# Modulating x instead of the weights and biases, loading the first operands by halves, and summing the gate row four slices at a time

## The chip, the cores and the metric

One core of a Trainium2 chip runs the whole layer. The metric is device time in microseconds (us), the median over several executions; the trace is one further execution under the hardware profiler.

## The reference

One hybrid decoder layer on x (4096 x 1024), cut to what matters here:

```
shift, scale, gate = split(silu(c) @ W_ada + b_ada)      # three rows of 1024
h = x * (1 + scale) + shift                              # adaLN modulation
p = h @ W_in                                             # W_in is 1024 x 3712
u = gelu(p[:, 0:512]); v = gelu(p[:, 512:1024]); g = p[:, 1024:1536]
A = u * (causal mix over chunks of 128 of groupwise LayerNorm(v)) * silu(g)
r, k, v, gate_b, wd, ad = token_shift(p[:, 1536:])       # t + mu * (previous t - t)
B = rwkv7(r, k, v, wd, ad) * silu(gate_b)
y = LayerNorm(alpha * x + gate * (concat(A, B) @ W_out))
```

## The kernel before

x comes transposed (xT), so that a matmul contracts over the 1024 features, in eight slices of 128 (KD = 8). Time is cut into 16 blocks of 256 steps (T). Each float32 operand is split into a rounded high part (ScalarE copy, L258) and the remainder (GpSimd or VectorE subtract, L259), and a product takes several matmuls: `gemm` (L381) makes per slice one of 128x512 (high weight against both halves of x) and one of 128x256 (low weight against high x); `added` (L390) joins the two sums.

The work has three stages. **Stage A** (`group_a`, 16 blocks) makes from x the parts that need no recurrence: four blocks of u, two half blocks of v (`psv`, L619 to L621), four of g (`w_g`), four of the gate of B (`w_gb`), one of decay and rate (`w_wd`), and at the end the spatial mix (`pM`, L667), whose results leave through `oa` (L672, L675). While a block runs, generators are advanced beside it (`alongside`): `weights` for block 0; `ada_gate`, which sums the gate row, for blocks 1 and 2; `stash`, which prepares later weights and puts them into DRAM, from block 3; `load_b` for block 15. **Stage B** runs the recurrence over two groups of heads, its order on the engines written out by `Weave`; it reads back the split x that stage A stored (`xhl`). The last stage multiplies by W_out (`pso`).

In stage A the order of instructions on each engine, the SyncE DMA queue included, is set by the framework before the run, from program order and modelled readiness; buffers of one tag are handed out in rotation. The tags that matter: `st` in `hpool` (3 buffers: loads of x, weights, gate slices), `wst` in `apool` (3), `w` in `w2` (6 of 8 KB per partition), `hl` in `hpool` (5: split x).

The modulation is never applied to x. `mod` holds shift in columns 0 to 7 and 1 + scale in columns 8 to 15. Each weight block is multiplied by 1 + scale on load (L285, L422, L533/534, L559), and shift times the weights becomes a bias: `group_row` (L340) sums a slice with a weight of 32 columns, on one quarter of the array's columns for each k % 4, `set_bias` (L261) turns that row into a column, and the bias goes into the activations (L400, L601, L642, L863) or is added (`bvb`, L624). At the beginning the four 1 MB loads of `w_ada` for scale come first, then W_in for u and x; those for shift come after the u products have begun. `ada_gate` loads one 128x512 slice of `w_ada` a step and sums the one before it.

Of the kernel before, what the change touches and what calls it, by code (L numbers as in the profile page):

```python
# [209 lines left out]
def hybrid_layer(ctx: ExitStack, tc: tile.TileContext, x, xT, w_ada, b_gate, w_in, cols,  # L210
# [43 lines left out]
    bias = cp_.tile([P, 25], F32, name="bias")  # L254
# [14 lines left out]
    def fetch_w(c0, name, nb, pool=None, eng=g, pools=None):  # L269
# [10 lines left out]
        def finish():  # L280
            pq = ps_m.tile([P, P], F32, tag="m", name="pbias")
            for q, st in enumerate(sts):
                for k in range(4):
                    group_row(pq, mod, 4 * q + k, st[:, k])
                v.tensor_tensor(st, st, mod[:, 8 + 4 * q:12 + 4 * q].unsqueeze(2).to_broadcast([P, 4, P]), op=ALU.mult)  # L285
                split(w[:, 0, 4 * q:4 * q + 4], w[:, 1, 4 * q:4 * q + 4], st, eng)
            set_bias(nb, pq)
            if nb >= 8:
                v.tensor_tensor(halo[:, nb - 8:nb - 7], omm[:, nb - 8:nb - 7], bias[:, nb:nb + 1], op=ALU.mult)
# [8 lines left out]
    def load_parts(src, i, keep=None):  # L298

        parts = []  # L300

        def quarters():
            kept = []
            for q in range(4):
                st = hpool.tile([P, 2, T], F32, tag="st", name="hst", bufs=3)
                ld(st, src[q * 256:(q + 1) * 256, i * T:(i + 1) * T].rearrange("(k p) t -> p k t", p=P))
                hl = hpool.tile([P, 2, 2, T], F32R, tag="hl", name="hx")
                split(hl[:, 0], hl[:, 1], st)
                parts.extend(hl[:, :, k] for k in range(2))
                kept.append(hl)  # L310
                yield
            if keep is not None:
                for q, hl in enumerate(kept):
                    ld(keep[:, q], hl.bitcast(F32))

        return parts, quarters()
# [29 lines left out]
    def ada_gate():  # L346
        for q in range(2):
            qs = slice(q * 512, (q + 1) * 512)
            pq = ps_l.tile([P, 512], F32, tag="l", name="pq")
            gst = []  # L350

            def fetch(k):
                st = hpool.tile([P, 512], F32, tag="st", name="gst", bufs=3)
                ld(st, w_ada[k * P:(k + 1) * P, 2 * D + q * 512:2 * D + (q + 1) * 512])
                gst.append(st)
# [18 lines left out]
    def load_all(src, i, keep=None):  # L374
        parts, steps = load_parts(src, i, keep)
        for _ in steps:
            pass
        return parts


    def gemm(h, w, spare=False):  # L381
        shape = [P, 2, T]
        ps = ps_s.tile(shape, F32, tag="s", name="psd") if spare else ps_d.tile(shape, F32, tag="d", name="psd")
        for k in range(KD):
            both = h[k]
            pe.matmul(ps, w[:, 0, k], both, start=(k == 0), stop=(k == KD - 1), skip_group_check=True)  # L386
            pe.matmul(ps[:, 0], w[:, 1, k], both[:, 0], start=False, stop=(k == KD - 1), skip_group_check=True)  # L387
        return ps
# [7 lines left out]
    def shift(ps, blk, pool, dst):  # L396
# [3 lines left out]
        s.activation(pv[:, 1:T + 1], ps, AF.Identity, scale=col(V_MU, blk), bias=bias[:, 8 + blk:9 + blk])  # L400
# [10 lines left out]
    def stash():  # L411
        for p in range(2):
            for nm, o in (("k", 512), ("r", 0), ("v", 1024)):
                c0 = o + (2 + p) * P
                pq = ps_m.tile([P, P], F32, tag="m", name="pbias")
                for q in range(2):
# [3 lines left out]
                    for k in range(4):  # L420
                        group_row(pq, mod, 4 * q + k, st[:, k])
                    v.tensor_tensor(st, st, mod[:, 8 + 4 * q:12 + 4 * q].unsqueeze(2).to_broadcast([P, 4, P]), op=ALU.mult)  # L422
                    stash_parts(wps[nm, p], q, st.rearrange("p k c -> p (k c)"))
                    yield
                later_bias(8 + c0 // P, pq)
# [17 lines left out]

    def later_bias(nb, pq):
        set_bias(nb, pq)
        v.tensor_tensor(halo[:, nb - 8:nb - 7], omm[:, nb - 8:nb - 7], bias[:, nb:nb + 1], op=ALU.mult)
# [17 lines left out]
    def load_b(ph):  # L464

        late = None
        for p in range(2):
            for nm, o in (("k", 512), ("r", 0), ("v", 1024)):
                c0 = o + (2 * ph + p) * P
                R[ph, nm, p], fin_ = fetch_w(NA + c0, f"w_{nm}{p}", 8 + c0 // P)  # L470
                if late:
                    late()
                late = fin_
                yield
# [11 lines left out]
    with ExitStack() as actx:  # L486
# [4 lines left out]
        bvb = apool.tile([P, DA], F32, name="bvb", bufs=1)  # L491
# [24 lines left out]
        wa = [ada_cols(2), ada_cols(3)]  # L516
        ust = []
        for r in range(2):
            t_ = w2.tile([P, KD, 256], F32, tag="w", name=f"ust{r}")
            ld(t_, w_in[:, r * 256:(r + 1) * 256].rearrange("(k p) c -> p k c", p=P))  # L520
            ust.append(t_)
            if r == 0:
                x0 = load_all(xT, 0, xhl[0])
        for n in range(2):
            ada_sum(2 + n, wa[n])
        v.scalar_tensor_tensor(mod[:, 8:16], pm[:, 8:16], 1.0, V[:, V_BA + 8:V_BA + 16], op0=ALU.add, op1=ALU.add)
        wa = [ada_cols(0), ada_cols(1)]

        def u_block(b):
            st = ust[b // 2][:, :, (b % 2) * P:(b % 2 + 1) * P]  # L530
            w = wpool.tile([P, 2, KD, P], F32R, tag="w", name=f"w_u{b}")
            for k in range(KD):
                s.activation(w[:, 0, k], st[:, k], AF.Copy, scale=mod[:, 8 + k:9 + k])  # L533
                v.scalar_tensor_tensor(w[:, 1, k], st[:, k], mod[:, 8 + k:9 + k], w[:, 0, k].bitcast(F32),
                                       op0=ALU.mult, op1=ALU.subtract)
            wu.append(w)

        def weights():
            for b in range(4):
                u_block(b)  # L540
                yield
            for n in range(2):
                ada_sum(n, wa[n])
            v.tensor_tensor(mod[:, 0:8], pm[:, 0:8], V[:, V_BA:V_BA + 8], op=ALU.add)
            for b in range(4):
                pq = ps_m.tile([P, P], F32, tag="m", name="pbias")
                for k in range(KD):
                    group_row(pq, mod, k, ust[b // 2][:, k, (b % 2) * P:(b % 2 + 1) * P])
                set_bias(b, pq)
# [5 lines left out]
            pvb = ps_l.tile([P, DA], F32, tag="l", name="pvb")  # L555
            for k in range(KD):
                st = vst[k // 4][:, k % 4]
                group_row(pvb, mod, k, st)
                v.tensor_scalar(st, st, mod[:, 8 + k:9 + k], None, op0=ALU.mult)  # L559
# [738 lines left out]
```

## Time and profile before

| | |
|---|---|
| median of 3 runs | 2567.16 us (2561.15 to 2572.73) |
| the profiled execution's own time | 2566.92 us |
| its span in the trace | 2565.2 us |
| TensorE matmuls busy | 2426.9 us, 95% of the span |
| VectorE, ScalarE, GpSimd busy | 62%, 50%, 30% |
| the 16 blocks of stage A end (last `pM` begins) | 916.87 us |

Busy TensorE time counts overlapping matmuls by their modelled ends, so 95% is not 95% of its peak.

### The profile page before, as it was taken

The numbers are of one execution on the slowest core, as the hardware profiler recorded it, in microseconds if no ns is written. First come the engines' busy times: TensorE is split into PE (matmuls) and PEld (weight loads), VectorE is DVE, ScalarE is ACT, GpSimd is POOL, SyncE is SP. The second block draws the span as 40 slices with busy tenths as digits, with TensorE's granted clock in tenths as the row PEclk, the third lists the DMA queues.
The fourth block names the chain that finished last, engine by engine and source line by source line (L and its number), as shares of the span: only waits on it lengthen the run. The fifth ranks groups of instructions, "written<-read, shape, count | busy, mean of one in ns | idle before, by whom it ended". The sixth has DMA issues, their size and how long they took to land.

```text
span 2565.2 us, 58841 instructions
## 1 busy us (share of the span) xinstructions
PE 2426.9 (95%) x23144; PEld 2095.7 (82%) x23144; DVE 1585.1 (62%) x4222; ACT 1277.6 (50%) x2963; POOL 768.3 (30%) x1419
## 2 busy tenths in 40 slices
PE   6999999999999989999999989999999998899998
PEld 3767888888888878888888888888988887688887
DVE  3733444434344457878778877778877787555555
ACT  3524444444443456676666656766766665211111
POOL 1412233322221242333233333333333333222221
PEclk8999999999999999999999999999999999999999
DMA  8423434543232252222122252222221224344442
GB/s 283 140 91 114 140 135 165 176 162 136 77 120 84 79 156 76 84 68 88 59 80 88 63 178 84 63 84 72 75 84 55 88 79 150 104 148 148 140 148 99
DMA packets 183102, 286.21 MB, mean 112 GB/s; under 512 B 14500, under 2 KB 125220, under 8 KB 181032
## 3 DMA queue, kind: packets, MB, share of 16 engines
q1 hardware_dynamic: 182824, 282.44, 33.7%
q8 instruction: 182, 2.98, 0.5%
q14 instruction: 96, 0.79, 0.1%
HBM read 188.00 MB, written 94.38 MB: 110 GB/s over the span
## 4 chain that ended last, share of the span: by engine, by line
PE 50%; DVE 15%; ACT 7%; issue 3%; DMA 2%; POOL 1%; SPq 0%; DVEq 0%; ACTq 0%; POOLq 0%
PE pso L1250 13%; PE psd L166 12%; PE psd L386 6%; PE pU L166 3%; PE pC L166 3%; PE psd L387 3%; PE pA L166 2%; DVE big L166 2%; DVE X L166 2%; DVE tmp L166 2%; PE pY L166 1%; PE pt L166 1%; DVE S L166 1%; PE pG L166 1%; ACT pv L166 1%
## 5 line engine op out<-in xcount | busy, mean ns | idle before, releaser
L1250 PE MATMUL pso<-wo,hx 128*128 128x512 f32 x1440 | 330.1, 391 | 1.8 <-POOL hx L1250 1.3
L1250 PEld LDWEIGHTS pso<-wo,hx 128*128 128x128 f32 x1440 | 270.3, 188 | 60.2 <-POOL hx L1250 1.7
L166 PE MATMUL psd<-hx,w_v 128*128 128x256 f32 x1512 | 248.9, 291 | 8.2 <-DVE kt L166 5.5
L166 PE MATMUL psd<-hx,w_r 128*128 128x256 f32 x1512 | 249.7, 290 | 1.1 <-DVE kt L166 1.1
L166 PE MATMUL psd<-hx,w_k 128*128 128x256 f32 x1512 | 238.9, 299 | 5.2 <-DVE rt L166 5.1
L393 DVE TENSOR_TENSOR sum<-psd,sum 128x256 f32<-128x256 f32 x208 | 87.5, 421 | 205.1 <-ACT sum L392 204.7
L166 PEld LDWEIGHTS psd<-hx,w_v 128*128 128x128 f32 x1512 | 202.9, 190 | 13.7 <-DVE kt L166 7.0
L166 PEld LDWEIGHTS psd<-hx,w_k 128*128 128x128 f32 x1512 | 203.0, 198 | 8.2 <-DVE rt L166 6.7
L166 PEld LDWEIGHTS psd<-hx,w_r 128*128 128x128 f32 x1512 | 203.7, 190 | 4.3 <-DVE kt L166 1.7
L386 PE MATMUL psd<-hx,w_u 128*128 128x512 f32 x512 | 188.4, 410 | 6.8 <-POOL hx L259 6.8
L386 PE MATMUL psd<-hx,w_gb 128*128 128x512 f32 x512 | 182.6, 397 | 2.9 <-DVE sum L393 2.9
L386 PE MATMUL psd<-hx,w_g 128*128 128x512 f32 x512 | 183.6, 400 | 0.9 <-DVE vg L624 0.4
L1250 POOL TENSOR_TENSOR hx<-hst,hx 128x512 fp32r<-128x512 f32 x58 | 84.2, 1452 | 219.2 <-ACT hx L1250 217.3
L166 ACT ACTIVATE pv<-psd,bias,V 128x256 f32<-128x256 f32 x192 | 106.4, 564 | 79.9 <-PE psd L166 77.4
L387 PE MATMUL psd<-hx,w_u 128*128 128x256 f32 x512 | 145.4, 285 | 0.0
L387 PE MATMUL psd<-hx,w_gb 128*128 128x256 f32 x512 | 143.9, 281 | 0.0
L387 PE MATMUL psd<-hx,w_g 128*128 128x256 f32 x512 | 143.7, 281 | 0.0
L392 ACT COPY sum<-psd 128x256 f32<-128x256 f32 x208 | 76.0, 366 | 118.8 <-PE psd L387 118.7
L166 POOL COPY halo<-pv 128x1 f32<-128x1 f32 x192 | 40.2, 210 | 309.4 <-ACT pv L166 302.9
L1250 DVE SCALAR_TENSOR_TENSOR z<-z,pso 128x512 f32<-128x512 f32 x60 | 41.2, 686 | 146.8 <-PE pso L1250 146.7
L386 PEld LDWEIGHTS psd<-hx,w_u 128*128 128x128 f32 x512 | 98.4, 193 | 35.6 <-POOL hx L259 10.0
L386 PEld LDWEIGHTS psd<-hx,w_g 128*128 128x128 f32 x512 | 96.1, 188 | 30.5 <-issue 5.1
(309 smaller groups left out, 5947.5 us busy)
## 6 DMA issues: line engine op xcount, KB each, us to landing
hx<-xhl SPq DMA_DIRECT2D x126, 512.0 KB, 4.1
xhl<-hx SPq DMA_DIRECT2D x64, 512.0 KB, 3.0
hst<-in_xT_dram SPq DMA_DIRECT2D x64, 256.0 KB, 3.1
hst<-oT SPq DMA_DIRECT2D x64, 256.0 KB, 2.9
z<-in_x_dram SPq DMA_DIRECT2D x32, 512.0 KB, 3.6
out_dram<-z SPq DMA_DIRECT2D x32, 512.0 KB, 2.6
wst<-in_w_in_dram SPq DMA_DIRECT2D x42, 256.0 KB, 3.0
wa<-in_w_ada_dram SPq DMA_DIRECT2D x8, 1024.0 KB, 9.5
```

The source lines that it names most:

```text
L166: fn(*a, **k)
L386: pe.matmul(ps, w[:, 0, k], both, start=(k == 0), stop=(k == KD - 1), skip_group_check=True)
L387: pe.matmul(ps[:, 0], w[:, 1, k], both[:, 0], start=False, stop=(k == KD - 1), skip_group_check=True)
L392: s.copy(t_, ps[:, 1])
L393: v.tensor_tensor(t_, ps[:, 0], t_, op=ALU.add)
L1250: fn(*a, **k)
```

## The change

x is multiplied by 1 + scale and shift is added, in place, before it is split (`modulate`: one `tensor_scalar` for each of the two slices of a quarter of x). The weights are split as they are, and every bias, `set_bias`, `later_bias`, the group rows for biases and `bvb` are gone; `pv` becomes a Copy with a scale. The start loads by halves of the contraction: `first_half(a)` loads scale and shift for 512 features, two quarters of x and 512 rows of the u weights; `second_half(a)` splits them, sums scale and shift and modulates. The four u products run over slices 0 to 3, and after the second half over 4 to 7. In `group_a` the g products come ahead of the v products. `ada_gate` loads four slices in one step and sums all four in the next.

```diff
-    def set_bias(nb, pq):
-        rows = hpool.tile([P, P], F32, tag="rows", name="brow", bufs=1)
-        s.copy(rows, pq)
-        pb_ = ps_m.tile([P, 1], F32, tag="m", name="pb_")
-        pe.matmul(pb_, rows, row32, start=True, stop=True)
-        v.tensor_copy(bias[:, nb:nb + 1], pb_)
...
         def finish():
-            pq = ps_m.tile([P, P], F32, tag="m", name="pbias")
             for q, st in enumerate(sts):
-                for k in range(4):
-                    group_row(pq, mod, 4 * q + k, st[:, k])
-                v.tensor_tensor(st, st, mod[:, 8 + 4 * q:12 + 4 * q].unsqueeze(2).to_broadcast([P, 4, P]), op=ALU.mult)
                 split(w[:, 0, 4 * q:4 * q + 4], w[:, 1, 4 * q:4 * q + 4], st, eng)
-            set_bias(nb, pq)
...
+    def modulate(q, st):
+        for k in range(2):
+            c = 2 * q + k
+            v.tensor_scalar(st[:, k], st[:, k], mod[:, 8 + c:9 + c], mod[:, c:c + 1], op0=ALU.mult, op1=ALU.add)
+        hl = hpool.tile([P, 2, 2, T], F32R, tag="hl", name="hx")
+        split(hl[:, 0], hl[:, 1], st)
+        return hl
...
-            for k in range(KD + 1):
-                if k < KD:
-                    fetch(k)
-                if k > 0:
-                    group_row(pq, sg1, k - 1, gst[k - 1])
-                yield
+            for k0 in (0, 4):
+                gst = []
+                for k in range(k0, k0 + 4):
+                    if k % 4 == 3:
+                        st = hpool.tile([P, 512], F32, tag="st", name="gst", bufs=3)
+                    else:
+                        st = pool.tile([P, 512], F32, tag="wst", name="gst2", bufs=3)
+                    ld(st, w_ada[k * P:(k + 1) * P, 2 * D + q * 512:2 * D + (q + 1) * 512])
+                    gst.append(st)
+                yield
+                for k in range(k0, k0 + 4):
+                    group_row(pq, sg1, k, gst[k - k0])
                 yield
...
+    def load_all(i):
+        hls = [modulate(q, fetch_x(i, q)) for q in range(4)]
+        keep_parts(i, hls)
+        return slices(hls)
...
-        s.activation(pv[:, 1:T + 1], ps, AF.Identity, scale=col(V_MU, blk), bias=bias[:, 8 + blk:9 + blk])
+        s.activation(pv[:, 1:T + 1], ps, AF.Copy, scale=col(V_MU, blk))
...
+        def first_half(a):
+            wa = [ada_cols(2 + a), ada_cols(a)]
+            xs = [fetch_x(0, 2 * a), fetch_x(0, 2 * a + 1, apool.tile([P, 2, T], F32, tag="wst", name="hst3", bufs=3))]
+            st = w2.tile([P, 4, 512], F32, tag="w", name=f"ust{a}")
+            ld(st, w_in[a * 512:(a + 1) * 512, 0:512].rearrange("(k p) c -> p k c", p=P))
+            half[a] = wa, xs, st
+
+        def second_half(a):
+            wa, xs, st = half[a]
+            for b in range(4):
+                split(wu[b][:, 0, 4 * a:4 * a + 4], wu[b][:, 1, 4 * a:4 * a + 4], st[:, :, b * P:(b + 1) * P], (g, v)[b % 2])
+            for n, q in enumerate((2 + a, a)):
+                ada_sum(q, wa[n])
+            ...
+            return [modulate(2 * a + n, x_) for n, x_ in enumerate(xs)]
...
+        first_half(0)
+        hl0 = second_half(0)
+        first_half(1)
...
+                for b in range(4):
+                    dense(pus[b], slices(hl0), wu[b], 0, 4)
+                hl0.extend(second_half(1))
+                h = slices(hl0)
+                yield
+                for b in range(4):
+                    dense(pus[b], h, wu[b], 4, KD)
+                    gelu_u(pus[b])
+                    yield
...
-                v.tensor_tensor(vg2, ps, bvb, op=ALU.add)
-                s.activation(vg2, vg2, AF.Gelu_apprx_tanh)
+                s.activation(vg2, ps, AF.Gelu_apprx_tanh)
...
-            yield ac.activation(pv[:, 1:T + 1], ps, AF.Identity, scale=col(V_MU, blk), bias=bias[:, 8 + blk:9 + blk])
+            yield ac.activation(pv[:, 1:T + 1], ps, AF.Copy, scale=col(V_MU, blk))
```

## Rows read from the trace of the kernel before

**Rows 1.** The page: busy time of each engine, and the chain that ended last.
```profile
PE 2426.9 (95%) x23144; PEld 2095.7 (82%) x23144; DVE 1585.1 (62%) x4222; ACT 1277.6 (50%) x2963; POOL 768.3 (30%) x1419
...
PE pso L1250 13%; PE psd L166 12%; PE psd L386 6%; PE pU L166 3%; PE pC L166 3%; PE psd L387 3%; PE pA L166 2%; DVE big L166 2%; DVE X L166 2%; DVE tmp L166 2%; PE pY L166 1%; PE pt L166 1%; DVE S L166 1%; PE pG L166 1%; ACT pv L166 1%
```

**Rows 2.** Busy time by stretch; each stretch runs from one block's `pM` to the next's.
```profile
114.50:179.52 65.02, 63.86 (x313) 43.98 (x312) 21.63 (x69) 20.93 (x42) 9.48 (x21) 1.00 0.31 100
179.52:241.31 61.79, 58.16 (x302) 45.10 (x301) 20.79 (x67) 23.61 (x45) 14.15 (x21) 0.94 0.33 109
241.31:294.67 53.36, 52.32 (x324) 43.34 (x323) 23.05 (x72) 24.76 (x50) 17.00 (x26) 1.00 0.42 143
...
401.44:452.80 51.36, 50.40 (x292) 42.69 (x291) 23.16 (x72) 23.52 (x48) 16.96 (x26) 1.00 0.49 169
...
706.29:756.23 49.94, 49.94 (x290) 42.59 (x289) 20.37 (x66) 22.06 (x44) 11.76 (x22) 1.00 0.26 90
...
856.09:916.87 60.78, 58.24 (x397) 45.87 (x396) 35.36 (x90) 27.52 (x59) 27.75 (x32) 1.00 0.41 132
```

**Rows 3.** Timeline of the first block: start, duration, engine, line, what, count.
```profile
9.83 1.93 PE L342 MATMUL pq<-wa,sg 128*32 128x512 f32 x8 [9.83 <-DMA wa<-in_w_ada_dram]
...
23.35 0.17 DVE L526 SCALAR_TENSOR_TENSOR mod<-pmod,V 128x8 f32<-128x8 f32 x1 [1.96 <-PE pmod L513]
...
26.44 0.79 PE L386 MATMUL psd<-hx,w_u 128*128 128x512 f32 x1 [3.13 <-POOL hx L259]
...
28.53 0.63 PE L386 MATMUL psd<-hx,w_u 128*128 128x512 f32 x1
...
29.17 0.64 PE L386 MATMUL psd<-hx,w_u 128*128 128x512 f32 x1
...
40.16 1.06 PE L342 MATMUL pq<-wa,sg 128*32 128x512 f32 x8
...
114.50 1.97 PE L667 MATMUL pM<-wm,vg 128*64 128x128 f32 x32
```

**Rows 4.** TensorE's groups from 0 to 122 us: the sums for the biases after u and v.
```profile
L342 PE MATMUL pbias<-wst,mod 128*32 128x128 f32 x144 | 6.2, 280 | 0.0
```

**Rows 5.** Busy time, 0 to 20 us (last columns: granted clock, DMA share, GB/s).
```profile
0.00:10.00 10.00, 0.17 (x4) 0.20 (x8) 0.39 (x4) 1.49 (x2) 0.46 (x8) 1.00 0.80 270
10.00:20.00 10.00, 8.50 (x40) 2.55 (x35) 0.69 (x1) 0.00 (x0) 0.00 (x0) 1.00 1.07 379
```

**Rows 6.** Timeline of 700 to 760 us, blocks 11 and 12, several engines.
```profile
711.72 1.28 ACT L601 ACT_TABLE_LOAD   x1
...
714.16 1.51 SPq L306 DMA_DIRECT2D hst<-in_xT_dram  x3
...
715.28 0.41 DVE L675 TENSOR_TENSOR oa<-oa,sl 128x256 f32<-128x256 f32 x1
...
742.79 0.42 DVE L393 TENSOR_TENSOR sum<-psd,sum 128x256 f32<-128x256 f32 x1 [2.39 <-ACT sum L392]
745.59 0.42 DVE L393 TENSOR_TENSOR sum<-psd,sum 128x256 f32<-128x256 f32 x1 [2.38 <-ACT sum L392]
...
756.79 2.52 POOL L259 TENSOR_TENSOR hx<-hst,hx 128x512 fp32r<-128x512 f32 x2
```

**Rows 7.** Groups of 0 to 1020 us: the gate row's sums and the cast of x.
```profile
L258 ACT CAST hx<-hst 128x512 fp32r<-128x512 f32 x64 | 38.0, 615 | 26.0 <-DMA hst<-in_xT_dram 22.2 <-PE psd L387 3.8
...
L342 PE MATMUL pq<-gst,sg 128*32 128x512 f32 x32 | 15.7, 604 | 1.2 <-DMA gst<-in_w_ada_dram 1.2
```

**Rows 8.** Groups of 856 to 917 us, block 15.
```profile
L342 PE MATMUL pbias<-wst,mod 128*32 128x128 f32 x96 | 4.9, 283 | 2.3 <-DMA wst<-in_w_in_dram 2.3
```

**Rows 9.** Instructions on `mod`: ns least, median, most; first and last start.
```profile
L559 DVE TENSOR_SCALAR vst<-vst,mod x8: 473/484/1529, 57.7 to 65.0; 128x512 f32<-128x512 f32 x8
```

**Rows 10.** ScalarE's groups of stage B, 930 to 2170 us.
```profile
L166 ACT ACTIVATE pv<-psd,bias,V 128x256 f32<-128x256 f32 x192 | 106.4, 564 | 79.9 <-PE psd L166 77.4 <-POOL wua L166 0.5 <-issue 0.2
...
L166 ACT ACTIVATE sa<-pw,nwa 128x256 f32<-128x256 f32 x128 | 55.9, 470 | 1.6 <-PE pw L166 1.2
```

More of the change, by code (lines that the diff above doesn't have):

```diff
@@ L296, in load_w, with fetch_x, slices, keep_parts @@
         return w
[L298 to L310, printed above, removed]
-                yield
[L312 to L316, printed above, removed]
+    def fetch_x(i, q, st=None):
+        if st is None:
+            st = hpool.tile([P, 2, T], F32, tag="st", name="hst", bufs=3)
+        ld(st, xT[q * 256:(q + 1) * 256, i * T:(i + 1) * T].rearrange("(k p) t -> p k t", p=P))
+        return st
+    def modulate(q, st):
[5 more added lines that the diff above has]
+        return hl
+    def slices(hls):
+        return [hl[:, :, k] for hl in hls for k in range(2)]
+    def keep_parts(i, hls):
+        for q, hl in enumerate(hls):
+            ld(xhl[i][:, q], hl.bitcast(F32))
     def reload_parts(i, spare=()):
@@ L372, in ada_gate, with dense @@
             yield
[L374 to L384, printed above, removed]
+    def load_all(i):
+        hls = [modulate(q, fetch_x(i, q)) for q in range(4)]
+        keep_parts(i, hls)
+        return slices(hls)
+    def dense(ps, h, w, k0, k1):
+        for k in range(k0, k1):
             both = h[k]
@@ L527, in hybrid_layer @@
[L527 to L536, printed above, removed]
+        half = [None, None]
@@ new lines, in first_half @@
+        def first_half(a):
[10 more added lines that the diff above has]
+                ada_sum(q, wa[n])
+            sc, sh = slice(8 + 4 * a, 12 + 4 * a), slice(4 * a, 4 * a + 4)
+            v.scalar_tensor_tensor(mod[:, sc], pm[:, sc], 1.0, V[:, V_BA + sc.start:V_BA + sc.stop], op0=ALU.add,
+                                   op1=ALU.add)
+            v.tensor_tensor(mod[:, sh], pm[:, sh], V[:, V_BA + sh.start:V_BA + sh.stop], op=ALU.add)
+            return [modulate(2 * a + n, x_) for n, x_ in enumerate(xs)]
@@ L538, in weights @@
+        for b in range(4):
+            wu.append(wpool.tile([P, 2, KD, P], F32R, tag="w", name=f"w_u{b}"))
+        first_half(0)
+        hl0 = second_half(0)
+        first_half(1)
         def weights():
             for b in range(4):
-                u_block(b)
+                wgt.append(load_w(2 * DA + b * P, f"w_g{b}", None if b < 3 else w2, (g, v)[b % 2], (None, apool)[b % 2]))
                 yield
-            for n in range(2):
-                ada_sum(n, wa[n])
-            v.tensor_tensor(mod[:, 0:8], pm[:, 0:8], V[:, V_BA:V_BA + 8], op=ALU.add)
@@ L545, in weights @@
[L545 to L549, printed above, removed]
             vst = []
@@ L687, in hybrid_layer @@
         next(wgen)
-        next(wgen)
         alongside(first, wgen)
+        for _ in wgen:
+            pass
         for i in range(1, NSB):
             if i == 1:
-                gate_steps = ada_gate()
+                gate_steps = ada_gate(apool)
                 later = stash()
```

91 lines of the change are left out of this document (27 added, 64 removed).

## The prediction

> **What bounds the kernel now.** I read the page first: TensorE is busy 95% of the span, and the chain that ended last is half TensorE [rows 1]. So I asked of each stretch how much of it is products that must be made, and how much is something else. For that I cut stage A at each `pM`, the last products of a block, and asked for busy time by stretch [rows 2]. Blocks 10 to 14 take 49.94 us each, and TensorE has no idle time in them: 13 products of 2.80 us, the spacing of two `sum` rows [rows 6], are 36.4; `pM` is 1.97 [rows 3]; the v products are the rest, 11.6. 49.94 us is the floor of a block, and whatever a block takes above it is excess: 15.1 and 11.9 us in blocks 1 and 2, 3.4 in each of blocks 3 to 5, 1.4 in block 6, 10.8 in block 15 [rows 2]. Then I read the timeline of block 0 [rows 3]. Its first product begins at 26.44, the u products end at 40.16, and `pM` begins at 114.50. After u only 9 products and v are left, 25.2 + 11.6 = 36.8 us of work, but 74.3 us go by. 37.5 us of that stretch are bias sums, shift sums, waits and slow pace.
>
> **The start.** It is 4 MB of `w_ada` that the first product waits for now (scale alone), and it is 4 MB after the change (scale and shift for half the features). The row that sums them begins at 9.83 and `mod` is written at 23.35 [rows 3]; I keep that time. x then needs two `tensor_scalar` before its cast, of at most 0.48 us each, the median for twice the columns [rows 9]; the weights, free of `mod`, can be split earlier. First product: 26.5 to 28, say 27.
>
> The first half is 4 products of 4 slices. Now a slice takes 0.64 us at the beginning (28.53 to 29.17) [rows 3], and later 2.80/8 = 0.35 [rows 6]; eight slices at each pace give 7.9 us, to 35. The second half brings 5.5 MB more. The first 10 us move 2.7 MB (270 GB/s), and at the 379 GB/s of the next 10 [rows 5] all 11.4 MB land by about 33, its shift and scale by about 29. Its two sums take TensorE some 3.5 us each (groups of 1.06 [rows 3], a copy and the turning into columns). Placed between the first products they end at 36, behind them at 42. Then modulate, cast (0.62 [rows 7]) and subtraction (1.26, half of the pair [rows 6]) are 2.9 us. So the second half starts at 39 to 45, say 41, takes 5.6 us at full pace and 10 at the slow one, and u ends between 46 and 56, say 49: later than now.
>
> What follows u is bare: 36.8 us, since the sums for the biases (6.2 us busy for nine blocks [rows 4], besides those for u and v, the turned rows and their waits) are gone. I add 5 us for weights that arrive late, since each block of 0.5 MB passes two of three buffers. `pM` at 91 instead of 114.5: **23.5 us**. Ends: u at 56 and 12 us of waits give 105 (9.5); u at 46 and none give 83 (31.5).
>
> **Blocks 1 and 2.** Their excess is 27 us [rows 2]. The 16 sums of gate slices, two instructions each, were made one at a time, 15.7 us busy, 0.98 a slice [rows 7]. Four slices together, on four quarters of the array's columns, took 1.06 us [rows 3]: four such groups are 4.2 us. Two row products of about 1 us (one gate sum's size) remain, and I allow 3 us of waits, since four loads are now due at once with one step to land in. All of it fits into block 1. Excess 9.4 instead of 27: **17.5 us**. Ends: 12 (waits of 8.5 us), 22 (5 us left). Buffers: the gate took `st` ten times a half, now four times, so x should no longer come late to block 2, in which TensorE idles 3.6 us [rows 2]; if it does, the gain is at the lower end.
>
> **Blocks 3 to 5.** `stash` loses its sums. Left is what block 6, which stashes W_out, shows above the floor: at worst 1.4, at best nothing, against 3.4. I take 0.6: **8.4 us** (6 to 10.2).
>
> **Block 15.** 96 sum instructions, 4.9 us busy, and 2.3 us of waits for them [rows 8] go, with six turned rows and changes of shape, out of 10.8 us of excess. Loads and splits stay, off TensorE. I take 1.8 left: **9 us** (6 to 10.8).
>
> **Every block.** x for the next block is requested long before its use: three quarters at 714.16, while the last splits are made at 756.79 [rows 6]. The eight `tensor_scalar` a block, under 0.48 us each [rows 9], need only the loaded buffer, not the `hl` buffer for which the splits wait. VectorE is busy 20.4 of 49.94 us [rows 2], and two additions of `bvb` leave it. I count them as nothing, hidden in those 40 us; without that cover they cost what the second rival says. ScalarE gets two more table loads a block, since u (gelu), g (silu) and v (gelu) now alternate; each is 1.28 us [rows 6] on an engine that is busy 22 of 50 [rows 2]. v now leaves PSUM by ScalarE; the third buffer gives it a product's time, 2.80 us, and more. Nothing again; the bound is 32 x 1.28 = 41 us if each stood in the path.
>
> **Stage B.** `pv` had a scale and a bias from columns, 564 ns; a like instruction with one such column takes 470 [rows 10]. 192 x 0.094 = 18 us of ScalarE, but only 1% of the chain is `pv` [rows 1], some 26 us or 45 instructions, so at most 4 to 6 us can come out. The order written by `Weave` stays, as it prices both forms alike. I take **3 us** (0 to 6).
>
> **A rule against the change.** One `tensor_scalar` took 1529 ns against a median of 484 [rows 9]. The Trainium skill, "SBUF — State Buffer", section "Summary: rules for kernel authors", says that when VectorE is in its mode with two ports, GpSimd and it do not overlap: the second to issue waits until the first has ended. The trace agrees in direction. By that rule each of the four modulations that gate a half at the start could stand behind a GpSimd subtraction of 1.26 us, 5 us in all, and the sum would be 2510.5; by the median it is 2505.5.
>
> **Sum.** 23.5 + 17.5 + 8.4 + 9 + 3 = 61.4 us, from the profiled execution's own 2566.9 us (0.2 below the median): 2505.5 us. All low ends give 2533, all high ends 2486.
>
> **Rivals.**
> - *The halves come too late.* The second half's sums stand on TensorE ahead of first products that could run, and loads behind a blocked request: the start gains 5 us only, 2524. For it: the queue is in order, and one load of x in the second half needs a buffer that a split frees. Against: all 11 MB are due by 33 at the measured rate. 0.10.
> - *Modulation behind the previous block* (the other side). If the `tensor_scalar` of block i+1 stand on VectorE in program order, they follow `oa` of block i, which ends at 715.69 for a `pM` that ended at 708.26 [rows 2, 3, 6]: 7.4 us, then 2.4 us for modulate, cast and subtraction, nearly 10 us of idle TensorE in 15 blocks, 147 us, and 2653. It turns the sign from 4.1 us a block. Against: casts and requests of x already run ahead of their place in the program. 0.04.
> - *ScalarE into the path.* Two table loads and v's eviction cost 1 to 2.6 us a block: 2521 to 2547. Against: 28 us of free time. 0.07.
> - *The gate still waits.* Blocks 1 and 2 keep their 27 us, the four loads being late together: 2523. For it: TensorE idles there now, too. 0.07.
> - *No change*, the savings being eaten by new waits of any kind: about 2560. 0.04.
>
> **How the numbers follow.** My forecast has 0.68; its own range is 2488 to 2528. With the late start, the gate and most of the ScalarE case the range is 2486 to 2536. This kernel can be told from no change at about 0.5%, 13 us. All cases but the second rival and the last lie below 2554: faster 0.91, same 0.05, slower 0.04.
>
> **What would show it.** `pM` of block 0 near 91 and the second half's first product near 41; block 2 at 50 to 52 us and block 1 at 56 to 60; blocks 3 to 5 near 50.5, block 15 near 52; blocks 10 to 14 still at 49.9, with `tensor_scalar` rows some 30 us ahead of their use; `pv` near 470 ns. I am wrong if blocks 10 to 14 lengthen, or if TensorE waits for `w_g` or `wv` after u.

## The result and the profile after

The kernel after takes 2541.69 us (median of 4 runs, 2538.61 to 2542.69), the kernel before on the same chip 2569.94 us (2561.15 to 2577.47): a ratio of 0.9889, 95% interval 0.9855 to 0.9924. It is faster, by 28 us or 1.1%, but it lies above the predicted range of 2486 to 2536. The profiled execution took 2542.27 us with a span of 2540.6 us, 24.6 us below the span of before.

I read the page of after first. TensorE is as busy as before [rows 1], so the forecast isn't to be checked there; the chain has three new members that are no engine.

```profile
PE 2392.1 (94%) x22676; PEld 2085.9 (82%) x22676; DVE 1564.3 (62%) x4199; ACT 1267.4 (50%) x2946; POOL 769.4 (30%) x1423
...
PE pso L1220 13%; PE psd L166 11%; PE psd L370 8%; PE psd L371 4%; PE pU L166 3%; PE pC L166 3%; DMA gt<-gate_row 2%; PE pA L166 2%; DVE big L166 2%; DVE X L166 2%; DVE tmp L166 2%; DVE S L166 1%; DMA wps_o<-whi 1%; PE pY L166 1%; DMA hst<-in_xT_dram 1%
```

The load of the gate row, the store of a stashed weight and the load of x now stand in the chain of what ended last. Next, as before [rows 2], busy time by stretch from one block's `pM` to the next's (length; busy us and count of PE, PEld, DVE, ACT, POOL; granted clock, DMA share, GB/s):

```profile
101.81:160.71 58.90, 58.24 (x325) 43.39 (x324) 24.05 (x74) 22.62 (x45) 11.77 (x21) 1.00 0.40 134
160.71:211.07 50.36, 50.27 (x289) 42.59 (x289) 23.76 (x74) 23.29 (x46) 11.97 (x21) 1.00 0.26 91
211.07:261.09 50.02, 50.02 (x289) 42.59 (x288) 22.09 (x72) 25.04 (x50) 16.93 (x25) 1.00 0.45 153
414.82:469.08 54.26, 51.18 (x289) 42.48 (x288) 23.93 (x75) 24.93 (x50) 16.82 (x24) 1.00 0.49 161
469.08:524.57 55.49, 52.28 (x290) 43.80 (x289) 23.90 (x75) 24.65 (x50) 16.80 (x24) 0.97 0.46 157
...
680.78:730.80 50.02, 50.02 (x290) 42.59 (x289) 21.99 (x72) 23.18 (x46) 11.86 (x21) 1.00 0.26 90
830.84:880.86 50.02, 50.02 (x290) 42.59 (x289) 18.52 (x64) 27.69 (x55) 24.73 (x31) 1.00 0.54 167
```

The first three rows are blocks 1 to 3, the next two are blocks 7 and 8, the last two are 12 and 15. Block 1 carries both halves of the gate; blocks 2, 3, 12 and 15 stand at the floor; 7 and 8 are 4 to 5.5 us above it, where before they were at 50.7 and 50.5. Summed by stage, from the first `pM` of each block (us):

| stretch | before | after | gain | forecast |
|---|---|---|---|---|
| to the first `pM` | 114.5 | 101.8 | 12.7 | 23.5 |
| blocks 1 and 2 | 126.8 | 109.3 | 17.5 | 17.5 |
| blocks 3 to 5 | 160.1 | 150.7 | 9.4 | 8.4 |
| blocks 6 to 10 | 254.9 | 269.0 | -14.1 | 0 |
| blocks 11 to 14 | 199.7 | 200.1 | -0.4 | 0 |
| block 15 | 60.8 | 50.0 | 10.8 | 9 |
| last `pM` to the end (stage B and output) | 1648.3 | 1659.7 | -11.4 | 3 |
| sum | 2565.2 | 2540.6 | 24.6 | 61.4 |

Three rows are off: the start, blocks 6 to 10, and stage B. The first row scatters: the eleven other traces below that keep the start as changed have their first `pM` at 98.7 to 104.8. The start in the timeline of block 0 (against [rows 3]):

```profile
20.96 1.86 PE L491 MATMUL pmod<-K,rows 128*128 128x1 f32 x8 [0.81 <-DVE rows L489]
25.92 0.80 PE L370 MATMUL psd<-hx,w_u 128*128 128x512 f32 x1 [3.10 <-POOL hx L259]
28.82 0.58 PE L371 MATMUL psd<-hx,w_u 128*128 128x256 f32 x1 [2.10 <-POOL w_u L259]
...
36.65 2.78 PE L329 MATMUL pq<-wa,sg 128*32 128x512 f32 x24
...
46.46 0.79 PE L370 MATMUL psd<-hx,w_u 128*128 128x512 f32 x1 [3.09 <-POOL hx L259]
49.36 0.58 PE L371 MATMUL psd<-hx,w_u 128*128 128x256 f32 x1 [2.11 <-POOL w_u L259]
...
57.12 0.40 PE L370 MATMUL psd<-hx,w_g 128*128 128x512 f32 x1
...
101.81 1.97 PE L636 MATMUL pM<-wm,vg 128*64 128x128 f32 x32
```

and busy time of the second half's u products, in the columns of the table of stretches above:

```profile
46.46:57.12 10.66, 8.55 (x33) 6.99 (x34) 8.93 (x8) 8.05 (x17) 10.21 (x7) 0.63 0.56 167
```

Three things are to be seen. The second half's sums (36.65) come behind all first-half products, and each half has a second wait of 2.1 us for the remainder of its weights: ScalarE casts x before it casts `w_u`, though nothing but the load holds the weights up (they landed at 21.4 and 36.5, and their casts begin at 25.07 and 45.61). Then the second half runs at a granted clock of 0.63: TensorE has no work from 43.4 to 46.5, its granted clock falls at 44.1, and until 54.4 it is at 1.2 GHz, the lower of its two levels.

### The profile page after: what moved, and what is told of

Same layout as the page of the kernel before. It is cut to its first block, busy times and chain, and to the rows that moved or that the text cites. A ratio compares the mean times of both kernels' runs of the same rounds, so it can differ in the third digit from the quotient of the medians.

```text
span 2540.6 us, 57950 instructions
## 1 busy us (share of the span) xinstructions
PE 2392.1 (94%) x22676; PEld 2085.9 (82%) x22676; DVE 1564.3 (62%) x4199; ACT 1267.4 (50%) x2946; POOL 769.4 (30%) x1423
## 3 DMA queue, kind: packets, MB, share of 16 engines
q8 instruction: 178, 2.92, 0.5%
## 4 chain that ended last, share of the span: by engine, by line
PE 55%; DVE 18%; ACT 7%; DMA 7%; issue 4%; POOL 2%; SPq 0%; DVEq 0%; ACTq 0%; POOLq 0%
PE pso L1220 13%; PE psd L166 11%; PE psd L370 8%; PE psd L371 4%; PE pU L166 3%; PE pC L166 3%; DMA gt<-gate_row 2%; PE pA L166 2%; DVE big L166 2%; DVE X L166 2%; DVE tmp L166 2%; DVE S L166 1%; DMA wps_o<-whi 1%; PE pY L166 1%; DMA hst<-in_xT_dram 1%
## 5 line engine op out<-in xcount | busy, mean ns | idle before, releaser
L166 PE MATMUL psd<-hx,w_v 128*128 128x256 f32 x1512 | 251.0, 293 | 13.0 <-DVE kt L166 5.5
L166 ACT ACTIVATE pv<-psd,V 128x256 f32<-128x256 f32 x192 | 89.9, 474 | 101.1 <-PE psd L166 97.7
L370 PEld LDWEIGHTS psd<-hx,w_gb 128*128 128x128 f32 x512 | 97.6, 191 | 35.9 <-ACT vg L601 8.6
```

Source lines behind the costliest of these rows:

```text
L166: fn(*a, **k)
```

## The experiments

All edits are to the kernel after, but for two to the kernel before. The letters of the theories are those of each expectation alone. "B" is the stretch from the last `pM` to the end. A ratio is to the kernel before, run on the same chip (its medians there are 2563.09 to 2566.49 us); a run without a ratio is a single execution.

### Stage B: where the code of TensorE lies

The order on every engine in stage B is the same before and after, and `pv` is as forecast, 474 ns against 564 [rows 10]:

```profile
L166 ACT ACTIVATE pv<-psd,V 128x256 f32<-128x256 f32 x187 | 87.6, 474 | 100.0 <-PE psd L166 97.0 <-POOL yo L166 0.7 <-POOL kt L166 0.2
```

Still B is longer. TensorE's timeline of after, in three units that follow each other (first fence), and busy time around the middle one's stall (second) show the kind of place:

```profile
1957.77 1.04 PE L166 MATMUL pA<-AR,BK 64*128 64x128 f32 x13
1960.49 0.49 PE L166 MATMUL pA<-AR,BK 64*128 64x128 f32 x3 [1.68 <-issue]
...
2000.27 0.93 PE L166 MATMUL pA<-AR,BK 64*128 64x128 f32 x10
2003.00 0.90 PE L166 MATMUL pA<-AR,BK 64*128 64x128 f32 x6 [1.80 <-issue]
...
2044.71 0.71 PE L166 MATMUL pA<-AR,BK 64*128 64x128 f32 x7
2047.84 1.43 PE L166 MATMUL pA<-AR,BK 64*128 64x128 f32 x9 [2.42 <-issue]
```

```profile
1985.00:2001.20 16.20, 14.87 (x247) 13.41 (x245) 15.13 (x44) 8.72 (x24) 6.12 (x14) 1.00 0.40 123
2001.20:2003.00 1.80, 0.00 (x1) 0.00 (x1) 0.34 (x2) 1.30 (x4) 0.38 (x1) 1.00 0.09 22
2003.00:2013.70 10.70, 10.70 (x114) 9.56 (x115) 4.92 (x10) 4.66 (x12) 2.00 (x5) 0.52 0.17 51
```

TensorE stops for 1.80 us in the middle of a row of like matmuls and waits for nothing that the profile shows ("issue"); then its granted clock is 0.52 for 10.7 us, nearly all of them at 1.2 GHz. Before, the same unit of work has its stall elsewhere:

```profile
2037.17 0.34 PE L166 MATMUL pG<-xd,am 32*32 32x32 f32 x9
2038.54 0.56 PE L166 MATMUL pG<-xd,am 32*32 32x32 f32 x23 [1.03 <-issue]
```

From 1834 to 2132 us the stalls of after come once in each unit of stage B, and from one unit to the next three matmuls earlier in the unit: 13, 10 and 7 `pA` products stand ahead of the three shown, and 509 matmuls lie from one stall to the next. Before 1834 us there are only three. In the kernel before it is the same from 1877 to 2116 us, in `pG`. Two runs add matmuls of 32x32 in block 12, which compute nothing that is used, so that the code behind them moves:

```diff
+    def pad(n):
+        pp = ps_m.tile([P, 8, 32], F32, tag="m", name="pp")
+        for j in range(n):
+            r_ = slice(32 * (j % 4), 32 * (j % 4) + 32)
+            pe.matmul(pp[r_, j // 4 % 8], K[r_, 0:32], K[r_, 0:32], start=True, stop=True,
+                      tile_position=(32 * (j % 4), 32 * (j % 4)))
...
+            if i == 12:
+                pad(52)      # kernel after; pad(12) in the kernel before
```

> The changed kernel with 52 tiny matmuls (32x32, their result unused) put ahead of the last products of block 12, which only shift where every later TensorE instruction lies in the code. Theory C (stage B lost time because TensorE stalls between two instructions of its code, at places that moved when the change took matmuls out): the shift carries the stalls of units 24 to 30 from the pA products back to the pG products, where the kernel before has them; stage B shortens from 1659.7 us to about 1648, less at most 5 for the faster pv; total about 2530 (block 12 longer by 1 to 2). Theory P (the faster pv itself shifts work on ScalarE so that TensorE idles): stage B stays at 1660 and the total at 2543.

Measured: 2519.45 us, ratio 0.9842 (0.981 to 0.9873) to before; B 1632.6, more than either theory expected and 27 us less than in the trace of after, by 52 matmuls more, which the trace counts as 104. The trace is of the shortest of the four executions; the medians differ by 22 us, on two chips. The stalls are back in `pG` and shorter:

```profile
2024.91 0.28 PE L166 MATMUL pG<-xd,am 32*32 32x32 f32 x5
2025.83 0.63 PE L166 MATMUL pG<-xd,am 32*32 32x32 f32 x27 [0.64 <-issue]
```

> The kernel before, with 12 tiny matmuls ahead of the last products of block 12: its code moves by 48 instructions. Theory C: the stalls of units 24 to 30 move from the pG products to the pA products, where the changed kernel has them, and stage B lengthens from 1648 us towards 1660; total about 2580. Theory P: no change, 2567 to 2570.

Measured: 2578.85 us, ratio 1.0062 (1.0042 to 1.0082); B 1657.0 against 1648.3, and the stalls of before now lie in `pA` and the products ahead of it, 1.3 to 2.2 us long for most. The place of the code moves the stalls in both directions.

The rival was `pv`: a faster ScalarE that shifts the work of others.

```diff
-            yield ac.activation(pv[:, 1:T + 1], ps, AF.Copy, scale=col(V_MU, blk))
+            yield ac.activation(pv[:, 1:T + 1], ps, AF.Identity, scale=col(V_MU, blk), bias=zb)
```

> The changed kernel with pv of stage B as Identity with a scale and a column of zeros as bias, as before; the TensorE code is the same instruction for instruction. Theory P: pv back at 564 ns, stage B back at 1648 us, total 2531. Theory C: stage B stays near 1660 or grows by up to 5 us, total 2542 to 2547, with the stalls at the same pA products.

Measured: 2539.16 us, ratio 0.9911 (0.9882 to 0.994), B 1654.7, stalls still in `pA`: the rival falls. Both edits together:

> The 52 tiny matmuls of a_pad52, and pv of stage B as Identity with a column of zeros as bias, as before the change; the TensorE code is that of a_pad52. If the faster pv is worth something where the code's stalls are out of the way, stage B goes from 1633 back to 1640 to 1648 us and the total from 2519 to 2527 or more. If a_pad52 only fell on a good place of the code, both stay: 1633 and 2519.

Measured: 2533.54 us, ratio 0.9871 (0.984 to 0.99); its profiled execution took 11561.56 us, so no stage B can be read from it. Against 0.9842 with the fast `pv` the intervals overlap.

What TensorE waits for is in the DMA view. First the whole of after, then 2000.4 to 2001.7, the end of a burst in which x is loaded for the next unit (packets, MB, share of 16 engines):

```profile
q1 hardware_dynamic: 181800, 282.44, 34.2%
q8 instruction: 178, 2.92, 0.5%
```

```profile
DMA packets 255, 0.23 MB, mean 175 GB/s; under 512 B 24, under 2 KB 228, under 8 KB 254
...
q1 hardware_dynamic: 254, 0.21, 47.9%
q8 instruction: 1, 0.02, 4.5%
```

2.92 MB in 178 packets are 16.4 KB each, and they come all through the run. One begins at 2000.66 and takes 0.94 us; TensorE goes on at 2003.00. The packet before it came 17.5 us earlier and the next 3.6 us later, where four a unit of 43 us would be one in 11: it came late, as the burst ended. It is so at each of the 17 stalls above 0.2 us between 1500 and 2200 us in the two traces: a packet of that queue ends 1.2 to 1.6 us ahead of the first matmul behind the stall, and in the 6 us before that packet the DMA engines were busy for 54 to 97%, against 27% from 1500 to 2200 us in after. The Trainium skill, "Runtime: NRT & Kernel Launch", section "Instruction fetch mechanics", says that an engine's sequencer fetches its code in blocks of 16 KiB over a DMA queue of its own while it runs the block before, at a cost that is mostly hidden. The trace agrees on size and way; hidden it is not at these 17 places, where the block is due within a burst of other loads.

Stalls and lost clock account for B. Summed from the last `pM` on: stalls put down to "issue", and one minus the granted clock over slices of 2 us:

| kernel | stalls | lost clock | B | B without both |
|---|---|---|---|---|
| before | 8.8 | 35.4 | 1648.3 | 1604.1 |
| after | 18.3 | 40.0 | 1659.7 | 1601.4 |
| `a_pad52` | 6.9 | 23.4 | 1632.6 | 1602.3 |
| `a_vfirst` (below) | 13.6 | 30.4 | 1646.5 | 1602.5 |
| `a_sums` (below) | 16.0 | 48.9 | 1664.9 | 1600.0 |
| `a_pvid` | 13.3 | 29.6 | 1654.7 | 1611.9 |
| `b_pad12` | 13.7 | 33.4 | 1657.0 | 1609.8 |

Without both, after is 2.7 us shorter than before, near the 3 us that were forecast for `pv`, but one pair doesn't settle the size: the 15 traces with the fast `pv` have 1596 to 1605 (mean 1601.4), the four with the slow one 1604 to 1612 (mean 1607.9), 6.5 us apart. B also scatters: the versions that keep the number of matmuls ahead of B as in after have 1646 to 1665. In these the stalls are 13.1 to 18.3 us, against 6.5 and 8.8 in the two traces with the code of before, so the stalls go with the code; the lost clock, 29.6 to 48.9 against 33.9 and 35.4, isn't told apart. So of the 11.4 us lost the longer stalls, 9.5 us between the two traces, are shown, and how much of the clock is this execution's stays open.

### Blocks 6 to 10: the stash of W_out

After the change VectorE waits longer for the gate row in these blocks. Its groups from 360 to 640 us, before and after (busy, mean ns, idle time ahead):

```profile
L433 DVE TENSOR_TENSOR wst<-wst,gt 128x512 f32<-128x512 f32 x16 | 11.1, 692 | 52.1 <-DMA gt<-gate_row 46.3 <-issue 4.4 <-POOL sl L643 1.4
```

```profile
L416 DVE TENSOR_TENSOR wst<-wst,gt 128x512 f32<-128x512 f32 x16 | 11.1, 692 | 73.0 <-DMA gt<-gate_row 73.0
```

TensorE itself waits longest for ScalarE's gelu of v (L601), which empties a PSUM buffer: 7.3 of the 11.4 us that it waits in blocks 6 to 10 of after (3.8 in before; total, times, longest):

```profile
PE psd L370 <- ACT vg L601: 7.3, 4, 2.8
```

Seven runs undo one part or one buffer each: v ahead of g again; v out of PSUM by a VectorE copy before its gelu; both together; the gate row in a buffer of `apool`; the modulation on ScalarE; three quarters of x in buffers of their own; and no modulation of x at all.

```diff
+            for part in (v_part, g_part) if i else (g_part, v_part):          # a_vfirst, a_noswitch
+                yield from part()
...
+                v.tensor_copy(vg2, ps)                                        # a_vcopy, a_noswitch
-                s.activation(vg2, ps, AF.Gelu_apprx_tanh)
+                s.activation(vg2, vg2, AF.Gelu_apprx_tanh)
...
-                gt = hpool.tile([P, 512], F32, tag="st", name="gt", bufs=3)
+                gt = state["apool"].tile([P, 512], F32, tag="wst", name="gt", bufs=3)      # a_gt
...
-            v.tensor_scalar(st[:, k], st[:, k], mod[:, 8 + c:9 + c], mod[:, c:c + 1], op0=ALU.mult, op1=ALU.add)
+            s.activation(st[:, k], st[:, k], AF.Identity, scale=mod[:, 8 + c:9 + c], bias=mod[:, c:c + 1])      # a_actmod
...
+            return state["apool"].tile([P, 2, T], F32, tag="wst", name="hst4", bufs=3) if i > 2 and q < 3 else None      # a_xwst
...
-        hls = [modulate(q, fetch_x(i, q)) for q in range(4)]
+        hls = [modulate(q, fetch_x(i, q), False) for q in range(4)]           # a_nomod: split only
```

> The changed kernel with the v products ahead of the g products again in blocks 1 to 15; all else as changed. Theory V (blocks 6 to 10 lengthened because v now comes late, when the stash's waits stand ahead of it on ScalarE, which alone empties its PSUM buffer): those five blocks fall from 269 us to about 256, TensorE's waits for the gelu of v are gone. Theory S (the stash's and x's loads share three buffers, and VectorE and ScalarE stand in order behind the loads that come late, whichever product is first): they stay at 265 or more, with the waits moved to other products.

> The changed kernel, but VectorE copies v out of PSUM and gelu runs from SBUF, as before the change; order and all else as changed. Theory V: blocks 6 to 10 at about 257. Theory S: VectorE itself stands 5 to 8 us behind the gate row's load, so the copy is late too; 264 or more.

> The changed kernel with the stash's copy of the gate row (gt) in the free wst buffers of apool, out of the three st buffers that x and the weights share. Theory S: VectorE's waits for gt shrink, and blocks 6 to 10 fall from 269 us to about 255. Theory V: v is still emptied by ScalarE alone and late; 264 or more.

> The changed kernel with the modulation of x on ScalarE (Identity with scale and bias columns) in place of VectorE's tensor_scalar. Theory M (the lengthening of blocks 6 to 10 comes from the new station on VectorE: it stands in order behind the loads of the gate row and of x, and the PSUM sums behind it are late): those blocks fall from 269 us to about 257, though ScalarE is busy some 4 us longer a block. Theory R (x's loads themselves come late, since x and the stash share three st buffers, whoever modulates): 265 or more.

> The changed kernel with three of the four quarters of x loaded into the free wst buffers of apool from block 3 on, out of the ring that the stash uses; modulation stays on VectorE. Theory R: x lands before the stash's loads, blocks 6 to 10 at about 255. Theory M: VectorE still stands behind the gate row's loads; 264 or more.

> Left out: x is not modulated in blocks 1 to 15 (it is split as it is loaded), so the output isn't the reference's; loads, splits and products stay. Theory M (the two modulations between a load of x and its split hold a buffer of the loads longer and stand on VectorE behind the wait for the gate row, and that is what lengthens blocks 6 to 10): blocks 6 to 10 take 252 to 257 us, as before the change (254.9), and the whole about 2527. Rival O (the place of the g and v products, and v's way out of PSUM by ScalarE, do it, whatever is done to x): they stay at 264 to 270, and the whole at 2540.

> In blocks 1 to 15 the v products come ahead of the g products again, and v leaves PSUM by VectorE (a copy) before its gelu, as in the kernel before: both parts are undone together, the modulation of x stays. Rival O (order and eviction jointly): blocks 6 to 10 take 253 to 258 us. Theory M (the modulation of x): 263 to 270, as each of the two alone (264.7 and 267.9).

One execution each:

| kernel | blocks 6 to 10 | whole |
|---|---|---|
| after | 269.0 | 2541.69 |
| `a_vfirst` | 264.7 | 2536.66 |
| `a_vcopy` | 267.9 | 2542.72 |
| `a_gt` | 269.4 | 2531.86 |
| `a_actmod` | 269.1 | 2535.39 |
| `a_xwst` | 264.3 | 2534.26 |
| `a_nomod` | 265.1 | 2526.78 |
| `a_noswitch` | 267.0 | 2542.1 |

All seven miss: none comes near 254.9 (the whole differs by B besides, which scatters as said). In `a_xwst` and `a_vfirst` blocks 3 to 5 are longer besides (157.8, 160.0); `a_xwst` begins the stash of W_out in block 5 already. In `a_gt`, where the gate row no longer takes one of the `st` buffers, VectorE waits for the row of W_out in its place, and a step still takes 6.8 us:

```profile
L416 DVE TENSOR_TENSOR wst<-wst,gt 128x512 f32<-128x512 f32 x16 | 12.0, 748 | 52.7 <-DMA wst<-in_w_out_dram 52.7
```

So the gate row's place in the `st` buffers alone isn't it. I asked next whether the gate itself does it: without its load and multiplication, and with the load made once for all 16 steps.

```diff
+        gts = []
+        for q in range(2):
+            gt = state["apool"].tile([P, 512], F32, tag="wst", name="gt", bufs=3)
+            ld(gt, gate_row[:, q * 512:(q + 1) * 512].partition_broadcast(P))
+            gts.append(gt)
...
-                gt = hpool.tile([P, 512], F32, tag="st", name="gt", bufs=3)
-                ld(gt, gate_row[:, q * 512:(q + 1) * 512].partition_broadcast(P))
...
-                v.tensor_tensor(st, st, gt, op=ALU.mult)
+                v.tensor_tensor(st, st, gts[q], op=ALU.mult)                  # a_gt2; a_nogt has none of these
```

> Left out: the rows of W_out are stashed without being multiplied by the gate, and the gate row isn't loaded for it; so the output isn't the reference's. Cast, subtraction and both stores of each of the 16 steps stay. Theory G (VectorE standing at the multiplication for the gate row, with all that is queued behind it, is what lengthens blocks 6 to 10): they fall to 250 to 253 us, as blocks 3 to 5 with the same step without a gate (50.2 a block), and the whole to about 2524. Rival S (loads and stores of the stash themselves): 262 or more.

> The two halves of the gate row are loaded once, into two buffers that nothing else uses in blocks 3 to 10, in place of one load a step; VectorE multiplies as before, and the output is the reference's. Theory G (the chain through the three buffers of the loads: W_out and gate row in, multiply, cast, subtract, two stores out, then the next step, four steps, and only then x of the next block): without the gate row's load in it, blocks 6 to 10 take 250 to 253 us (269.0), as without the gate, and the whole about 2524. Rival S (it is VectorE's multiplications or the stores): 262 or more.

Measured: `a_nogt` 2525.08 us with blocks 6 to 10 at 251.0; `a_gt2`, which still multiplies, 2523.38 us, ratio 0.9827 (0.9799 to 0.9854), at 251.5, below before. Blocks 7 and 8 of `a_gt2`, and VectorE's group:

```profile
411.37:461.39 50.02, 50.02 (x289) 42.59 (x289) 24.32 (x76) 24.96 (x50) 17.23 (x25) 1.00 0.44 153
461.39:511.41 50.02, 50.02 (x289) 42.59 (x289) 24.45 (x76) 25.55 (x50) 17.57 (x26) 1.00 0.44 153
```

```profile
L419 DVE TENSOR_TENSOR wst<-wst,gt 128x512 f32<-128x512 f32 x16 | 11.9, 746 | 26.9 <-DMA wst<-in_w_out_dram 26.9
```

The same multiplications, and 27 us of waiting in place of 73. It is the load of the gate row in each step. Without it two rows of W_out are multiplied one after the other, and the four of block 8 lie within 11.6 us (472.58 to 484.17), against 24.2 in after. VectorE's timeline of block 8 of after shows what such a wait holds up:

```profile
484.36 0.69 DVE L416 TENSOR_TENSOR wst<-wst,gt 128x512 f32<-128x512 f32 x1 [2.76 <-DMA gt<-gate_row]
...
492.00 0.69 DVE L416 TENSOR_TENSOR wst<-wst,gt 128x512 f32<-128x512 f32 x1 [4.34 <-DMA gt<-gate_row]
...
499.87 0.69 DVE L416 TENSOR_TENSOR wst<-wst,gt 128x512 f32<-128x512 f32 x1 [4.58 <-DMA gt<-gate_row]
...
508.60 0.69 DVE L416 TENSOR_TENSOR wst<-wst,gt 128x512 f32<-128x512 f32 x1 [7.70 <-DMA gt<-gate_row]
...
512.49 0.74 DVE L293 TENSOR_SCALAR hst<-hst,mod 128x256 f32<-128x256 f32 x2 [0.58 <-DMA hst<-in_xT_dram]
```

A step takes 8 us: gate row in (median 3.3 us to landing), multiply, cast, subtract, two stores out, and only then is one of the three `st` buffers free for the next gate row. Four steps fill 32 of 50 us, and x of the next block comes behind them through the same buffers and the same queue. While VectorE stands at 501 to 508 it cannot empty what ScalarE and TensorE wait on.

Why did before not lose it, with steps as long? Either its chain had slack, or it just fitted:

```diff
                 v.tensor_tensor(st, st, gt, op=ALU.mult)
+                v.tensor_tensor(st, st, gt, op=ALU.mult)
+                v.tensor_tensor(st, st, gt, op=ALU.mult)      # in the kernel before
```

> The kernel before, with each row of W_out multiplied by the gate three times in place of once (so the output isn't the reference's): 1.4 us more in each of the four steps of a block, 5.5 us a block, on VectorE, which idles half the time there. If the kernel before stood already at the limit of the same chain (its four steps and its x fill a block to within 1 us): blocks 6 to 10 go from 254.9 to 270 or more, and the whole is 15 to 20 us longer. If the chain had slack in it before: under 262.

Measured: blocks 6 to 10 take 272.6 us, 17.7 more, of 22.1 us added (32 multiplications of 0.69); the whole 2585.46 against 2566.46. It just fitted: four fifths of what was added came out as time. Block 8 of after is 4.8 us longer than block 7 of before, and 4.1 of them lie in the chain: 15.3 us in place of 12.2 from `pM` to the first multiplication, 24.2 in place of 23.3 for the next three. Which part of the change adds these 4 us is not settled; neither its modulation nor its order does so alone (without the modulation, in `a_nomod`, the first multiplication of block 8 still comes 15.3 us behind its `pM`).

### The start and the gate

```diff
         def first_half(a):
+            st = w2.tile([P, 4, 512], F32, tag="w", name=f"ust{a}")           # a_ust: u weights first
+            ld(st, w_in[a * 512:(a + 1) * 512, 0:512].rearrange("(k p) c -> p k c", p=P))
             wa = [ada_cols(2 + a), ada_cols(a)]
...
-        hl0 = second_half(0)
+        second_half(0)                                                        # a_sums
+        hl0 = half_x(0)
         first_half(1)
+        second_half(1)
...
-                hl0.extend(second_half(1))
+                hl0.extend(half_x(1))
```

> The changed kernel with the second half's sums of shift and scale, and its split of the u weights, put ahead of the first half's products in program order. If the late sums are what held the second half back (they ran from 36.7 to 43.4 us, behind all first products), the second half starts near 41 in place of 46.5, u ends near 52 in place of 57 and pM of block 0 begins near 96.5 in place of 101.8. If TensorE's work only changes places, u ends at 56 or later.

> The changed kernel with each half's u weights loaded first. ScalarE then splits them before mod is there, in place of behind x, and TensorE's two waits of 2.1 us for w_u and part of those for hx go; mod is written 2.6 us later, since 1 MB lands ahead of it. If the split of the weights behind x matters more: u ends near 54 in place of 57. If the loads bound the start: u ends at 57 or later.

> The gate row is summed one slice at a time again, as before the change; all else is as after it. If the one-at-a-time sums, and not the biases or the modulation, were the 17.5 us of blocks 1 and 2: these take 124 to 128 us (109.3 with four at a time, 126.8 before), and the whole is 15 to 19 longer, about 2558. If the gain came from what else left these blocks: under 115.

Measured: `a_sums` ends u at 58.4 (after: 57.3) in 2546.61 us: with the second half's sums ahead of the first half's products in the program, the work only changes its place. `a_ust` ends u at 54.3 and has its first `pM` at 98.3, 3.5 us earlier than after, in 2529.23 us. The end of u alone proves little, since it scatters from 54.2 to 58.1 in traces that keep the start as changed, with the first product at 23.9 to 26.4; from the first product to the end of u it is 27.5 us here and 30.0 to 32.1 there, and its `pM` lies 2.6 us ahead of their mean of 100.8. The wait behind the first product is gone:

```profile
26.75 0.80 PE L370 MATMUL psd<-hx,w_u 128*128 128x512 f32 x1 [3.09 <-POOL hx L259]
27.34 0.42 PE L371 MATMUL psd<-hx,w_u 128*128 128x256 f32 x1
```

`a_gate1`, which sums one slice at a time again, has 128.8 us in blocks 1 and 2 (109.3 after, 126.8 before), 2550.66 in all: the gain there is that of summing four slices at a time.

### The cures together

Gate row loaded once, u weights first, and 52 small matmuls:

> The three cures together: the gate row loaded once, the u weights requested ahead of scale and shift at the beginning, and 52 tiny matmuls in block 12 that move the code of stage B. If they add up as measured one by one: first pM at 98, blocks 1 to 10 at 511, stage B at 1633, in all some 2494 us; if the tiny matmuls' effect depends on more than the place of the code, stage B is at 1650 to 1660 and the whole at 2511 to 2521.

Measured: 2500.74 us, ratio 0.9742 (0.9716 to 0.9767), faster than the kernel before and 41 us below the median of after: first `pM` at 97.9, blocks 1 to 10 at 511.9, B 1638.9 (stalls 7.7, lost clock 30.0, the rest 1601.2). They add up but for 6 us in B.

## Why the prediction was right and wrong

61.4 us were forecast and 24.6 came, between the two traces; of the 36.8 that are missing 14.1 are in blocks 6 to 10, 14.4 in stage B and 10.8 at the start; the other rows came out 2.4 better than forecast.

- **Blocks 1 and 2, 3 to 5, block 15**: right, in place and size: 37.7 us of the forecast 34.9. The gate's 32 sums fell from 15.7 us busy [rows 7] to 5.3 (4.2 forecast), and block 2 went to the floor.
- **Every block** (0 forecast): right where nothing else runs beside a block: blocks 11 to 14 went from 49.9 to 50.0, with five table loads of 1.28 us each and modulation in them. The rival that puts the modulation behind `oa` falls, and so does the one that puts ScalarE into the path: where TensorE waits for ScalarE's gelu, in blocks 6 to 10, giving v's eviction back to VectorE (`a_vcopy`) leaves 267.9 of 269.0 us. Wrong in blocks 6 to 10, by 14.1 us. The step that failed is "I count them as nothing, hidden in those 40 us": it took VectorE's busy share in block 11, 20.4 of 49.94 us, for cover in every block. In block 6 the share is much the same, 23.16 of 51.36 us [rows 2], but there VectorE was idle because it stood in its queue, waiting for the gate row, and the chain through that wait filled the block already. The term for blocks 3 to 5 read block 6's excess of 1.4 us as the stash's cost; it was a chain with no slack left. A sign of it stood in the trace of before and wasn't taken up: block 9, with nothing but the stash beside it, took 52.55 us, 2.6 above the floor.
- **Stage B** (3 us): the term for `pv` is right in kind (2.7 us without stalls and lost clock between the two traces, 6.5 between the means of all), the step that an unchanged order gives unchanged time is wrong. Code was taken out ahead of stage B, so other matmuls stood where the next block of code came late.
- **The start** (23.5 us, measured 12.7, within the bounds of 9.5 to 31.5): the first product is right, 25.9 against 27. The term that was mis-sized is the second half: its first product came at 46.5, not 41 and 1.5 us past the late bound, its sums lying behind the first products, the later of the two places named; then 10.7 us to the end of u, not 8, most of it at the lower clock (the slow pace that the step had as its bound) and with 2.1 us for the weights' remainder, a wait that the step had ruled out ("can be split earlier"): they were loaded, but cast behind x. After u 44.7 us passed, not 41.8. The early bound of 46 for the end of u doesn't follow from its own terms, which give 39 + 5.6 = 44.6; that changes nothing here.
- **The rule against the change** (VectorE waiting behind GpSimd) could not show at the start, where it was weighed: GpSimd was idle until 24.59 and again until 45.13, behind both halves' modulations, and the four of a half took 1.38 us together. Later in the trace of after it does show. Of the 128 modulations the 11 that begin while GpSimd subtracts (L259) take 0.81 to 1.39 us, and each ends 0.15 us behind that subtraction; the other 117 take 0.32 to 0.42. All modulations (ns least, median, most; first and last start), and one of the 11, the third of these four:

```profile
L293 DVE TENSOR_SCALAR hst<-hst,mod x128: 321/409/1390, 23.1 to 798.4; 128x256 f32<-128x256 f32 x128
...
643.14 2.36 DVE L293 TENSOR_SCALAR hst<-hst,mod 128x256 f32<-128x256 f32 x4
643.68 1.35 POOL L259 TENSOR_TENSOR hx<-hst,hx 128x512 fp32r<-128x512 f32 x1 [6.95 <-ACT hx L258]
```

  Blocks 11 to 14 have one such modulation each and stand at 50.0 us, so it cost no time there.

## What to carry to other kernels

Read an idle engine's waits before you use its idle time as cover: an engine that stands in its queue behind a load covers nothing, and what is put behind it lengthens the chain. Where a small operand is loaded anew in every step of a chain through few buffers, load it once; here that was worth 17.5 us, more than the loss it cures. When code is added or removed, look at TensorE's waits for nothing in long unrolled stretches beside bursts of loads: they move with the code.

## What the runs showed of the hardware

I had not expected that 52 matmuls whose results nothing uses could save some 20 us of a stage behind them. A stall of 0.3 to 3.1 us with no wait in the profile stood where a 16 KB packet of the instruction queue landed late in a burst of loads, and the granted clock was 0.52 for the 10.7 us behind the one shown. An in-place modulation of 0.4 us on VectorE took up to 1.39 us when it began during a GpSimd subtraction.
